# Turning the gate columns round and sending small factors through DRAM in a hybrid decoder layer

## The chip, the cores and the metric

The kernel runs on one core of a Trainium2 chip, as one program. A core has a matrix engine (TensorE, PE in the profile; its weight loads are PEld), VectorE (DVE), ScalarE (ACT), GpSimd (POOL) and SyncE (SP), which here only issues DMA transfers. The metric is device time in microseconds of one execution, median of several runs; smaller is better. All data is 32-bit floating point. TensorE multiplies operands in a reduced format, `fp32r`, so each operand is split into a high and a low part, and a product is three matmuls: high x high, high x low, low x high.

## The reference

One layer for 256 tokens of width 2048. A normalised x is projected by one wide matrix, and its columns feed three groups of heads (LRU, mLSTM, MoBA), each closed by a SiLU gate; then an output projection, cross-attention into 256 memory tokens, and a last norm. Cut to what the change touches:

```python
h = rms_norm(x, mix_norm_g)            # x * rsqrt(mean(x*x)) * g, one factor a token
p = h @ w_in
(lru_x, lru_z, ml_u, ml_o, ml_z, ml_i, ml_f, mo_q, mo_k, mo_v, mo_z) = jnp.split(p, SPLIT_POINTS, axis=-1)
# mLSTM, 4 heads
ig = ml_i + bi;  lf = log_sigmoid(ml_f + bf)
b = cumsum(lf);  m = running maximum of (ig - b), later b + m        # per head, over tokens
s = (q @ k.T) * exp(d - m) ...;  hn = layer_norm(sigmoid(ml_o) * num / den) * norm_g
y_ml = hn * silu(ml_z)
# MoBA, 6 heads, 256 tokens: one block, so causal softmax attention with a distance penalty
y_mo = softmax(q @ k.T * scale - slope * dist) @ v * silu(mo_z)
x = x + concat(y_lru, y_ml, y_mo) @ w_out
x = x + cross_attention(rms_norm(x), rms_norm(mem))
```

## The kernel before

The weights are cut into groups of columns (lx, u0, u1, o0, o1, q0, q1, k0, k1, z0, v0, v1, z1, z2, then out0 to out3, ck, cq, cv and wo), and each group into chunks of up to 128 x 1024 numbers (512 KB), numbered through the program: o0 is 24 to 31, o1 32 to 39, q0 40 to 47, q1 48 to 55, k0 56 to 63, k1 64 to 71, z0 72 to 79, v0 and v1 to 95, z1 96 to 103, z2 104 to 107.

Each chunk passes three stages. `load(i)` (L152, its DMA at L164) brings it into one of four `raw` buffers, from SyncE's queue. `split(i)` (L167) makes `wh` on ScalarE (L189) and `wl` on VectorE (through `tt`, L140), in six buffers each. `mm(i)` (L235) multiplies. Groups of kind "W" hold the weights still and move 256 token columns through TensorE (L251, L252, L254), so the result has channels on partitions. Groups of kind "X" hold the tokens still and move up to 512 weight columns (L266, L267, L268), so the result has tokens on partitions. 

The main loop over chunks emits the splits up to four chunks ahead and the loads another four ahead of those, then `mm(i)`. After a group's last chunk `done(group)` puts generators in a queue (evacuations in front, longer work behind), and after each chunk `step()` runs one step of the queue. So side work on VectorE and ScalarE stands in a row with the splits, and every engine works in the order in which the program names its instructions; nothing reorders them.

The work around the change: `square` and `stats` (L375, L388) make each token's 1/rms from squares on ScalarE, sums on GpSimd and two products on TensorE (L391, L400). `lru_core` (L422) has exponentials at L441 and L442 and a square root at L449. `o_evac` (L500) makes sigmoids (L507) and the raw mLSTM gates `if`. `ml_conv` (L487) runs four taps for each tile, three of them on VectorE as `w<-w,vec,w`. `ml_gates` (L511) makes the logarithm of the forget gate by `log1p` (L343), transposes the gates on TensorE to 4 rows of 256 tokens (L542, L543), scans them for the sum and the maximum (L545, L547) and transposes back (L556, L557); in the trace this begins at 138 us, in the chunks of q1. `ml_heads` spreads a head's maximum over partitions by matmuls with `nrow` (L610). `ml_z` and `mo_z` evacuate the SiLU gates, `ml_y` and `mo_y` multiply with them, in channels.

Of the kernel before, what the change touches and what calls it, by code (L numbers as in the profile page):

```python
# [97 lines left out]
def kernel(ctx: ExitStack, tc: tile.TileContext, xT, memT, x, mem, ws, vec_d, lw_d, fg_d, out):  # L98
# [274 lines left out]
    sq = {}  # L373

    def square(which, j):  # L375

        t = staged[which, j]
        if j == 0:
            sq[which] = small("mask", 512)
            S.activation(sq[which], t.rearrange("p a b -> p (a b)"), AF.Square)  # L380
        else:
            q = small("yt", 512)
            S.activation(q, t.rearrange("p a b -> p (a b)"), AF.Square)  # L383
            G.tensor_tensor(sq[which], sq[which], q, OP.add)  # L384
        if j == 7:
            G.tensor_tensor(sq[which][:, :256], sq[which][:, :256], sq[which][:, 256:], OP.add)

    def stats(which):  # L388
        p = ps()
        for t in range(2):  # L390
            P.matmul(p[:, t:t + 1], sq[which][:, t * 128:t * 128 + 128], ones[:, 0:1], start=True, stop=True)  # L391
# [2 lines left out]
        rstd_of(r, p[:, 0:2], D, RMS_EPS)
        d = small("yt", 512)[:, :256].rearrange("p (a b) -> p a b", a=2)
        for t in range(2):
            V.tensor_scalar(d[:, t, :], ident, r[:, t:t + 1], None, op0=OP.mult)
        yield
        p = ps()
# [732 lines left out]
```

## Time and profile before

| what | value |
|---|---|
| runs | 526.89, 526.77, 526.19 us |
| median | 526.77 us |
| the profiled execution | 527.48 us |
| its span in the trace | 525.8 us |
| TensorE's granted clock, mean | 0.995 |
| TensorE busy | 98% of the span |
| VectorE, ScalarE, GpSimd busy | 65%, 54%, 9% |

The trace covers 525.8 of the 527.48 us of its execution, and times in it count from the span's start. A row of a timeline has the start, the length, the engine, the line, the operation, what is written and read, the shape, a count, and in brackets how long the engine sat idle before it and who ended that. Lengths of TensorE's rows overlap, since its matmuls are pipelined: what a matmul costs is the distance from one start to the next. Where a helper such as `tt` makes the instruction, the line is the helper's, and the tile's name tells which one it is. Times of a chunk mean the start of its first matmul.

### The profile page before, as it was taken

The numbers are of one execution on the slowest core, as the hardware profiler recorded it, in microseconds if no ns is written. First come the engines' busy times: TensorE is split into PE (matmuls) and PEld (weight loads), VectorE is DVE, ScalarE is ACT, GpSimd is POOL, SyncE is SP. The second block draws the span as 40 slices with busy tenths as digits, with TensorE's granted clock in tenths as the row PEclk, the third lists the DMA queues.
The fourth block names the chain that finished last, engine by engine and source line by source line (L and its number), as shares of the span: only waits on it lengthen the run. The fifth ranks groups of instructions, "written<-read, shape, count | busy, mean of one in ns | idle before, by whom it ended". The sixth has DMA issues, their size and how long they took to land.

```text
span 525.8 us, 8864 instructions
## 1 busy us (share of the span) xinstructions
PE 514.1 (98%) x3498; PEld 485.3 (92%) x3498; DVE 339.3 (65%) x522; ACT 282.3 (54%) x424; POOL 47.6 (9%) x67
## 2 busy tenths in 40 slices
PE   7999999999999999999999999999999999999993
PEld 6999999999999999999999999888888899988883
DVE  5986937695567537376666775764667866337574
ACT  4864567578645323432556455544648564447343
POOL 7354000000000000000200000000142010000000
PEclk9999999999999999999999999999999999999998
DMA  8975445467454554634557326588685565633604
GB/s 290 340 266 183 155 119 156 151 199 239 134 187 165 168 161 151 201 108 134 154 177 268 111 95 225 175 295 302 204 277 164 197 199 172 204 110 122 228 13 160
DMA packets 30362, 96.73 MB, mean 184 GB/s; under 512 B 3312, under 2 KB 3696, under 8 KB 30320
## 3 DMA queue, kind: packets, MB, share of 16 engines
q1 hardware_dynamic: 30176, 96.02, 55.7%
q8 instruction: 27, 0.44, 0.3%
q14 instruction: 15, 0.12, 0.1%
q10 hardware_dynamic: 144, 0.14, 0.1%
HBM read 94.05 MB, written 2.10 MB: 183 GB/s over the span
## 4 chain that ended last, share of the span: by engine, by line
PE 53%; issue 41%; DMA 2%; POOL 1%; DVE 1%; ACT 0%; POOLq 0%; ACTq 0%; SPq 0%; DVEq 0%
PE acc_out L266 6%; PE acc_out L268 6%; PE acc_out L267 6%; PE acc_z L252 2%; PE acc_z L254 2%; PE acc_z L251 2%; PE acc_v L268 1%; PE acc_ck L254 1%; PE acc_cq L254 1%; PE acc_cq L252 1%; PE acc_cq L251 1%; PE acc_ck L252 1%; PE acc_ck L251 1%; PE acc_v L267 1%; PE acc_v L266 1%
## 5 line engine op out<-in xcount | busy, mean ns | idle before, releaser
L140 DVE TENSOR_TENSOR wl<-raw,wh 128x1024 fp32r<-128x1024 f32 (+3 forms) x166 | 197.3, 1198 | 100.6 <-ACT wh L189 99.0
L189 ACT ACTIVATE wh<-raw 128x1024 fp32r<-128x1024 f32 (+2 forms) x162 | 160.8, 1010 | 49.7 <-PE acc_k L252 12.8
L266 PE MATMUL acc_out<-wh,ah_y 128*128 128x512 f32 x128 | 50.8, 397 | 0.0
L268 PE MATMUL acc_out<-wh,al_y 128*128 128x512 f32 x128 | 49.9, 390 | 0.0
L267 PE MATMUL acc_out<-wl,ah_y 128*128 128x512 f32 x128 | 49.8, 389 | 0.0
L251 PE MATMUL acc_z<-ah_x,wh 128*128 128x256 f32 x160 | 46.6, 291 | 0.0
L254 PE MATMUL acc_z<-ah_x,wl 128*128 128x256 f32 x160 | 45.2, 283 | 0.0
L252 PE MATMUL acc_z<-al_x,wh 128*128 128x256 f32 x160 | 45.2, 283 | 0.0
L251 PE MATMUL acc_q<-ah_x,wh 128*128 128x256 f32 x128 | 37.2, 290 | 0.0
L251 PE MATMUL acc_k<-ah_x,wh 128*128 128x256 f32 x128 | 37.0, 289 | 0.0
L251 PE MATMUL acc_u<-ah_x,wh 128*128 128x256 f32 x128 | 36.8, 288 | 0.0
L254 PE MATMUL acc_u<-ah_x,wl 128*128 128x256 f32 x128 | 36.2, 283 | 0.0
L252 PE MATMUL acc_k<-al_x,wh 128*128 128x256 f32 x128 | 36.2, 283 | 0.0
L252 PE MATMUL acc_u<-al_x,wh 128*128 128x256 f32 x128 | 36.2, 283 | 0.0
L254 PE MATMUL acc_q<-ah_x,wl 128*128 128x256 f32 x128 | 36.2, 283 | 0.0
L254 PE MATMUL acc_k<-ah_x,wl 128*128 128x256 f32 x128 | 36.2, 283 | 0.0
L252 PE MATMUL acc_q<-al_x,wh 128*128 128x256 f32 x128 | 36.2, 283 | 0.0
L384 POOL TENSOR_TENSOR mask<-mask,yt 128x512 f32<-128x512 f32 x14 | 22.4, 1598 | 152.6 <-ACT yt L383 152.6
L252 PEld LDWEIGHTS acc_z<-al_x,wh 128*128 128x128 f32 x160 | 30.6, 192 | 0.2
L251 PEld LDWEIGHTS acc_z<-ah_x,wh 128*128 128x128 f32 x160 | 30.6, 192 | 0.2
L254 PEld LDWEIGHTS acc_z<-ah_x,wl 128*128 128x128 f32 x160 | 30.6, 191 | 0.0
L268 PEld LDWEIGHTS acc_out<-wh,al_y 128*128 128x128 f32 x128 | 24.0, 188 | 5.1
(286 smaller groups left out, 1291.0 us busy)
## 6 DMA issues: line engine op xcount, KB each, us to landing
raw<-ws SPq DMA_DIRECT2D x138, 512.0 KB, 4.0
raw<-ws SPq DMA_DIRECT2D x24, 384.0 KB, 3.1
raw<-ws SPq DMA_DIRECT2D x8, 392.0 KB, 3.2
w<-x SPq DMA_DIRECT2D x4, 512.0 KB, 6.5
w<-memT SPq DMA_DIRECT2D x8, 256.0 KB, 4.9
out<-xg SPq DMA_DIRECT2D x8, 256.0 KB, 3.0
w<-xT SPq DMA_DIRECT2D x7, 256.0 KB, 6.2
raw<-ws SPq DMA_DIRECT2D x4, 256.0 KB, 5.6
```

Source lines behind the costliest of these rows:

```text
L140: V.tensor_tensor(out, a, b, op)
L189: S.activation(h[:, :kc * n], r[:, :kc * n], AF.Copy)
L251: P.matmul(o, h[:, sl], mv_h, start=first and m % 2 == 0, stop=False, skip_group_check=True)
L252: P.matmul(o, h[:, sl], mv_l, start=False, stop=False, skip_group_check=True)
L254: P.matmul(o, l[:, sl], mv_h, start=False, stop=last, skip_group_check=True)
L266: P.matmul(o, xh[:, sl], mh, start=first, stop=False)
L267: P.matmul(o, xh[:, sl], ml, start=False, stop=False)
L268: P.matmul(o, xl[:, sl], mh, start=False, stop=last)
L384: G.tensor_tensor(sq[which], sq[which], q, OP.add)
```

## The change

Five things are changed.

The gate groups z0, z1 and z2 (and the two gate tiles that were in k1) become kind "X": weights move, and the gates come out with tokens on partitions. `gate_z` evacuates them by ScalarE alone, with 1/rms as a scale. The heads' outputs are multiplied with them token by token, and `to_channels` transposes the products on TensorE, for MoBA too; MoBA's values are made token by token, with the softmax's division folded into their evacuation.

The sums of squares come from loads of x and mem by rows (`row_load`, four of 512 KB each), squared and summed along the row on ScalarE; 1/rms is written to DRAM (256 numbers) and read back broadcast to all partitions.

The mLSTM gates move from the queue to a list `side` that is advanced after every chunk, beginning right after o0. Their transposes are replaced by DMA through DRAM: `d_if` is written, two transfers of 4 x 256 single numbers read it as `gates_in`; after the scans two such transfers write `d_gates`, which is read back as `acol`; the maximum is broadcast as `nrow` (512 KB). All of them are issued from SyncE's queue.

At the start, the first half of x's first tile is issued ahead of the first weights, `vec` comes in two pieces, and the high part of x's second tile is made by ScalarE. The load of `lw` moves from chunk 3 to chunk 6, and the LRU's evacuation comes one step later.

The core of the diff:

```diff
-    ("k1", "w_in", "W", "x", _cols(*_t(O_K, 4, 5), *_t(O_Z, 0, 1))),
-    ("z0", "w_in", "W", "x", _cols(*_t(O_Z, 2, 3, 4, 5))),
+    ("k1", "w_in", "W", "x", _cols(*_t(O_K, 4, 5))),
+    ("z0", "w_in", "X", "x", [(O_Z, 512)]),
...
-    ("z1", "w_in", "W", "x", _cols(*_t(O_MZ, 0, 1, 2, 3))),
-    ("z2", "w_in", "W", "x", _cols(*_t(O_MZ, 4, 5))),
+    ("z1", "w_in", "X", "x", [(O_Z + 512, 256), (O_MZ, 256)]),
+    ("z2", "w_in", "X", "x", [(O_MZ + 256, 512)]),
...
-            if which == "x" and j < 2:
+            if which == "x" and j < 1:
...
+    stage_load("x", xT, 0, (0, 1))
+    nc.scalar.dma_start(vec[:, :16], vec_d[:, :16])
     load(0, (0,))
-    stage_load("x", xT, 0, (0, 1))
-    nc.scalar.dma_start(vec, vec_d)
...
+    nc.sync.dma_start(vec[:, 16:], vec_d[:, 16:])
...
-        p = ps()
-        for t in range(2):
-            P.matmul(p[:, t:t + 1], sq[which][:, t * 128:t * 128 + 128], ones[:, 0:1], start=True, stop=True)
...
-        P.matmul(p[:, :256], ones[:, :128], d.rearrange("p a b -> p (a b)"), start=True, stop=True)
...
+    def row_load(which, src, i, tag):
+        rows[which, i] = big(tag, 1024)
+        t, c = i // 2, i % 2 * 1024
+        nc.sync.dma_start(rows[which, i], src[t * 128:t * 128 + 128, c:c + 1024])
+
+    def row_square(which, i):
+        t = rows[which, i]
+        S.activation(t, t, AF.Square, accum_out=ssq[which][:, i // 2, i % 2:i % 2 + 1])
...
+        V.reduce_sum(r, ssq[which], axis=AX.X)
+        rstd_of(r, r, D, RMS_EPS)
+        yield
+        d = drp.tile([2, 128], F32, name=f"d_{which}")
+        with nc.allow_non_contiguous_dma(reason="two numbers a token"):
+            nc.sync.dma_start(d.rearrange("t p -> p t"), r)
+        yield
         rr = small("rrow", 256)
         rrow[which] = rr
-        S.activation(rr, p[:, :256], AF.Copy)
+        nc.sync.dma_start(rr, d.rearrange("t p -> (t p)")[None, :].to_broadcast([128, 256]))
...
+        d = drp.tile([256, 8], F32, name="d_if")
+        nc.sync.dma_start(d.rearrange("(t p) c -> p t c", t=2), iff)
+        yield
+        w = selp.tile([4, 2, 256], F32, name="gates_in")
+        with nc.allow_non_contiguous_dma(reason="one number each"):
+            for a in range(2):
+                nc.sync.dma_start(w[:, a, :], d[:, 4 * a:4 * a + 4].rearrange("n h -> h n"))
...
+        o = selp.tile([4, 3, 256], F32, name="gates_out")
+        av, cb, ncm = (o[:, i, :] for i in range(3))
+        V.tensor_tensor_scan(cb, ones[:4, :], w[:, 1, :], 0.0, op0=OP.mult, op1=OP.add)
...
+        d, dn = drp.tile([256, 8], F32, name="d_gates"), drp.tile([4, 256], F32, name="d_nrow")
+        with nc.allow_non_contiguous_dma(reason="one number each"):
+            for a in range(2):
+                nc.sync.dma_start(d[:, 4 * a:4 * a + 4].rearrange("n h -> h n"), o[:, a, :])
+        nc.sync.dma_start(dn, o[:, 2, :])
+        yield
+        ac, nrow = small("acol", 2, 8), selp.tile([128, 4, 256], F32, name="nrow")
+        nc.sync.dma_start(ac, d.rearrange("(t p) c -> p t c", t=2))
+        nc.sync.dma_start(nrow, dn[None, :, :].to_broadcast([128, 4, 256]))
...
-            pn = ps()
-            for i in range(2):
-                P.matmul(pn[:, :256], M["sel"][:, h, :], M["nrow"][i], start=i == 0, stop=i == 1)
+            pn = M["nrow"][:, h, :]
...
+    def gate_z(group, a):
+
+        if group == "z0":
+            M["sz"] = big(6, 2, 768)
+            parts = [(0, 512, M["sz"], 0)]
+        elif group == "z1":
+            B["sz"] = big(2, 2, 768)
+            parts = [(0, 256, M["sz"], 512), (256, 512, B["sz"], 0)]
+        else:
+            parts = [(0, 512, B["sz"], 256)]
+        for t in range(2):
+            for c0, c1, dst, d0 in parts:
+                S.activation(dst[:, t, d0:d0 + c1 - c0], a[t][:, c0:c1], AF.Silu, scale=rstd["x"][:, t:t + 1])
...
+    def to_channels(src, c):
+
+        p = ps()
+        for cc in range(2):
+            for t in range(2):
+                P.transpose(p[:, cc * 256 + t * 128:cc * 256 + t * 128 + 128],
+                            src[:, t, (c + cc) * 128:(c + cc) * 128 + 128], ident)
+        return p
...
+            P.matmul(p[:, 0:128], pt[:, 0:128], v[:, 0, vs], start=True, stop=True)
+            P.matmul(p[:, 128:256], pt[:, 128:256], v[:, 0, vs], start=True, stop=False)
+            P.matmul(p[:, 128:256], pt[:, 256:384], v[:, 1, vs], start=False, stop=True)
+            for t in range(2):
+                S.activation(o[:, t, vs], p[:, t * 128:t * 128 + 128], AF.Copy, scale=RS[h][:, t:t + 1])
...
+        for g in side:
+            next(g, None)
...
-            bg(idle(4), stats("x"), lru_evac(a), call(softplus_lam), lru_core())
+            bg(idle(2), stats("x"), lru_evac(a), call(softplus_lam), lru_core())
...
-            bg(ml_gates())
+            side.append(ml_gates())
...
+        if 2 <= i < 6:
+            row_load("x", x, i - 2, i - 1)
+        if i == 6:
             nc.sync.dma_start(lw, lw_d)
-        while nsq < 8 and nsq < i - 1:
-            square("x", nsq)
-            nsq += 1
+        if 6 <= i < 10:
+            row_square("x", i - 6)
```

The order of instructions, at the three places where the prediction's steps lie. VectorE, the end of o0, before: the split of chunk 34 is ahead of these rows, `w` are three taps of the convolution, `wl_1228` is the split of chunk 35, `if` are the two gate evacuations, then follow chunks 36 and 37.

```order
L143 SCALAR_TENSOR_TENSOR w_1222<-w_795,vec,w_1222 128x256 x3
L140 TENSOR_TENSOR wl_1228<-raw_1147,wh_1227 128x768
L143 SCALAR_TENSOR_TENSOR if<-acc_o_1088,rstd_x,vec 128x8
L143 SCALAR_TENSOR_TENSOR if<-acc_o_1089,rstd_x,vec 128x8
L140 TENSOR_TENSOR wl_1252<-raw_1167,wh_1251 128x768
L143 SCALAR_TENSOR_TENSOR w_1222<-w_795,vec,w_1222 128x256 x3
L140 TENSOR_TENSOR wl_1276<-raw_1186,wh_1275 128x768
```

The taps ahead of `if` are what moves here. VectorE after, from the split of chunk 35 (`wl_1211`) to that of chunk 36 (`wl_1235`) and the first row of the forget gate's logarithm:

```order
L142 TENSOR_TENSOR wl_1211<-raw_1134,wh_1210 128x768
L145 SCALAR_TENSOR_TENSOR if<-acc_o_1072,rstd_x,vec 128x8
L145 SCALAR_TENSOR_TENSOR if<-acc_o_1073,rstd_x,vec 128x8
L142 TENSOR_TENSOR wl_1235<-raw_1153,wh_1234 128x768
L145 SCALAR_TENSOR_TENSOR lf_e<-if 128x8
```

No taps stand ahead of `if` any more. Five short rows further on, the end of the logarithm, the copy into `if`, the first taps and the split of chunk 37 (`wl_1290`):

```order
L145 SCALAR_TENSOR_TENSOR lf_q<-lf_q,lf_s_1260 128x8 x6
L145 SCALAR_TENSOR_TENSOR lf_q<-lf_q,lf_s 128x8
L358 TENSOR_SCALAR lf<-lf_q 128x8
L145 SCALAR_TENSOR_TENSOR lf<-if,lf 128x8
L528 COPY if<-lf 128x2x4
L145 SCALAR_TENSOR_TENSOR w_1284<-w_779,vec,w_1284 128x256 x3
L142 TENSOR_TENSOR wl_1290<-raw_1173,wh_1289 128x768
```

The ten short instructions of the logarithm now stand between the splits of chunks 36 and 37, and the copy for the DMA behind them. VectorE after, from the split of chunk 40 to that of chunk 41, where before there were three taps alone:

```order
L142 TENSOR_TENSOR wl_1361<-raw_1238,wh_1360 128x1024
L542 SCALAR_TENSOR_TENSOR gates_out<-ones,gates_in 4x256
L142 TENSOR_TENSOR gates_out<-gates_in,gates_out 4x256
L544 SCALAR_TENSOR_TENSOR gates_out<-ones,gates_out 4x256
L545 TENSOR_SCALAR gates_out<-gates_out 4x256
L142 TENSOR_TENSOR gates_out<-gates_out 4x256
L145 SCALAR_TENSOR_TENSOR w_1284<-w_779,vec,w_1284 128x256 x3
L142 TENSOR_TENSOR wl_1389<-raw_1293,wh_1388 128x1024
```

The five instructions on the gates stand ahead of the taps and of split 41, and the first of them reads `gates_in`, which comes by DMA.

SyncE, before, from load 41 on (a load waits until its `raw` buffer is free):

```order
L164 DMA raw_1279<-ws 128x1024
L164 DMA raw_1301<-ws 128x1024
L164 DMA raw_1323<-ws 128x1024
L164 DMA raw_1345<-ws 128x1024
L164 DMA raw_1367<-ws 128x1024
```

Nothing but weights stands in this stretch of the queue. SyncE, after, from load 41 (`raw_1293`) to the broadcast of `nrow`, behind which load 47 follows; 4x256x1 are single numbers:

```order
L166 DMA raw_1293<-ws 128x1024
L532 DMA d_if<-if 128x2x8
L166 DMA raw_1317<-ws 128x1024
L537 DMA gates_in<-d_if 4x256x1 x2
L166 DMA raw_1342<-ws 128x1024
L166 DMA raw_1364<-ws 128x1024
L166 DMA raw_1392<-ws 128x1024
L551 DMA d_gates<-gates_out 4x256x1 x2
L552 DMA d_nrow<-gates_out 4x256
L166 DMA raw_1419<-ws 128x1024
L555 DMA acol<-d_gates 128x2x8
L556 DMA nrow<-d_nrow 128x1024
```

`gates_in` waits for `d_if`, and `acol` for `d_gates`, with the loads behind them in the same queue.

ScalarE, before, around the LRU's SiLU gate (L461) up to the square root (L449); the exponentials of L441 and L442 stand ahead of these rows:

```order
L189 ACTIVATE wh_1082<-raw_945 128x784
L461 ACT_TABLE_LOAD
L461 ACTIVATE w_1102<-w_1102 128x512
L189 ACTIVATE wh_1105<-raw_985 128x784
L189 ACTIVATE wh_1124<-raw_1021 128x784
L189 ACTIVATE wh_1143<-raw_1055 128x784
L449 ACT_TABLE_LOAD
L449 ACTIVATE w_1012<-w_1012 128x1024
```

Three splits alone stand between the SiLU and the square root here. ScalarE, after, the same place:

```order
L461 ACT_TABLE_LOAD
L461 ACTIVATE w_1086<-w_1086 128x512
L191 ACTIVATE wh_1089<-raw_963 128x784
L441 ACT_TABLE_LOAD
L441 ACTIVATE w_1029<-w_947,nsp_125 128x256
L442 ACTIVATE w_1030<-w_947,sp_124 128x256
L441 ACTIVATE w_1029<-w_947,nsp_125 128x256
L442 ACTIVATE w_1030<-w_947,sp_124 128x256
L191 ACTIVATE wh_1111<-raw_1003 128x784
L191 ACTIVATE wh_1130<-raw_1039 128x784
L191 ACTIVATE wh_1149<-raw_1070 128x768
L449 ACT_TABLE_LOAD
```

The second four exponentials have come behind the SiLU and have a table load of their own. The table load of the sigmoids (L507) further down carried the wait for `if` before; now the first sigmoid carries it.

## Rows read from the trace of the kernel before

**Rows 1.** The page, busy time of each engine, share of the span, instructions.

```profile
PE 514.1 (98%) x3498; PEld 485.3 (92%) x3498; DVE 339.3 (65%) x522; ACT 282.3 (54%) x424; POOL 47.6 (9%) x67
```

**Rows 2.** Waits of TensorE: line, waited for: us in total, times, longest.

```profile
PE acc_lx L251 <- ACT wh L180: 1.3, 1, 1.3
...
PE acc_lx L254 <- DVE wl L140: 0.9, 2, 0.5
```

**Rows 3.** Timeline of TensorE, a chunk of each kind: start, length, instruction.

```profile
116.07 0.28 PE L251 MATMUL acc_q<-ah_x,wh 128*128 128x256 f32 x1
...
118.81 0.28 PE L254 MATMUL acc_q<-ah_x,wl 128*128 128x256 f32 x1
...
335.72 0.39 PE L266 MATMUL acc_out<-wh,ah_y 128*128 128x512 f32 x1
...
339.80 0.39 PE L266 MATMUL acc_out<-wh,ah_y 128*128 128x512 f32 x1
```

**Rows 4.** Timeline of TensorE, first matmuls of chunks 36 and 37.

```profile
107.75 0.33 PE L266 MATMUL acc_o<-wh,ah_x 128*128 128x384 f32 x1
...
109.83 0.33 PE L266 MATMUL acc_o<-wh,ah_x 128*128 128x384 f32 x1
```

**Rows 5.** Timeline of ScalarE: exponentials, square root, sigmoids, split of chunk 36.

```profile
75.48 1.28 ACT L441 ACT_TABLE_LOAD   x1
...
78.39 0.84 ACT L189 ACTIVATE wh<-raw 128x784 fp32r<-128x784 f32 x1
...
90.33 1.28 ACT L449 ACT_TABLE_LOAD   x1 [2.62 <-DVE w L143]
...
102.13 1.28 ACT L507 ACT_TABLE_LOAD   x1 [5.90 <-DVE if L143]
...
104.37 0.84 ACT L189 ACTIVATE wh<-raw 128x768 fp32r<-128x768 f32 x1
```

**Rows 6.** Timeline of VectorE, from the gates `if` to the split of chunk 37.

```profile
101.83 0.35 DVE L143 SCALAR_TENSOR_TENSOR if<-acc_o,rstd_x,vec 128x8 f32<-128x8 f32 x2
105.25 0.96 DVE L140 TENSOR_TENSOR wl<-raw,wh 128x768 fp32r<-128x768 f32 x1 [3.06 <-ACT wh L189]
106.12 1.52 DVE L143 SCALAR_TENSOR_TENSOR w<-w,vec,w 128x256 f32<-128x256 f32 x3
107.56 0.95 DVE L140 TENSOR_TENSOR wl<-raw,wh 128x768 fp32r<-128x768 f32 x1
```

**Rows 7.** Timeline of TensorE: the statistics of x, and chunk 13 behind them.

```profile
43.45 0.50 PE L391 MATMUL ps<-ones,mask 128*128 128x1 f32 x4
43.82 0.36 PE L251 MATMUL acc_u<-ah_x,wh 128*128 128x256 f32 x1
...
46.77 0.60 PE L400 MATMUL ps<-yt,ones 128*128 128x256 f32 x2
47.02 0.47 PE L251 MATMUL acc_u<-ah_x,wh 128*128 128x256 f32 x1
```

**Rows 8.** The page, DMA queues (packets, MB, share) and issues (KB, us to landing).

```profile
q1 hardware_dynamic: 30176, 96.02, 55.7%
...
q10 hardware_dynamic: 144, 0.14, 0.1%
...
out<-xg SPq DMA_DIRECT2D x8, 256.0 KB, 3.0
```

**Rows 9.** Timeline of VectorE, the split of chunk 13.

```profile
36.40 1.67 DVE L140 TENSOR_TENSOR wl<-raw,wh 128x1024 fp32r<-128x1024 f32 x1 [0.57 <-ACT wh L189]
```

**Rows 10.** Timeline of VectorE: the logarithm, the split behind it, the scans.

```profile
138.49 0.16 DVE L143 SCALAR_TENSOR_TENSOR lf_e<-if 128x8 f32<-128x8 f32 x1
...
141.69 1.22 DVE L140 TENSOR_TENSOR wl<-raw,wh 128x1024 fp32r<-128x1024 f32 x1
...
150.71 0.68 DVE L545 TENSOR_TENSOR_SCAN w<-ones,ps 4x256 f32<-4x256 f32 x1 [1.45 <-PE ps L543]
...
153.24 0.27 DVE L551 CAST nrow<-w 4x256 fp32r<-4x256 f32 x1
```

More of the change, by code (lines that the diff above doesn't have):

```diff
@@ L372 @@
     rrow = {}
[L373 to L386, printed above, removed]
+    ssq = {w: small(f"ssq_{w}", 2, 2) for w in "xm"}
+    rows = {}
+    def row_load(which, src, i, tag):
[5 more added lines that the diff above has]
+        S.activation(t, t, AF.Square, accum_out=ssq[which][:, i // 2, i % 2:i % 2 + 1])
     def stats(which):
[L389 to L391 removed]
         r = small(f"rstd_{which}", 2)
         rstd[which] = r
[L394 to L397, printed above, removed]
+        V.reduce_sum(r, ssq[which], axis=AX.X)
+        rstd_of(r, r, D, RMS_EPS)
         yield
[L399 to L400 removed]
+        d = drp.tile([2, 128], F32, name=f"d_{which}")
+        with nc.allow_non_contiguous_dma(reason="two numbers a token"):
+            nc.sync.dma_start(d.rearrange("t p -> p t"), r)
+        yield
         rr = small("rrow", 256)
         rrow[which] = rr
[L403 removed]
+        nc.sync.dma_start(rr, d.rearrange("t p -> (t p)")[None, :].to_broadcast([128, 256]))
+        yield
+        yield
     def rb(which):
@@ L526, in ml_gates @@
                             channel_multiplier=-1)
-        w = big(6, 4, 256)[:4]
-        sel = selp.tile([128, 4, 128], F32R, name="sel")
-        ones_r = ones[:, :128]
-        M["sel"] = sel
-        for h in range(4):
-            G.affine_select(sel[:, h, :], ones_r, pattern=[[0, 128]], compare_op=OP.is_equal, fill=0.0,
-                            base=-h, channel_multiplier=1)
-        nrow = [selp.tile([128, 256], F32R, name=f"nrow{i}") for i in range(2)]
-        for r in nrow:
-            G.memset(r.bitcast(F32), 0.0)
@@ L537, in ml_gates @@
-        M["nrow"] = nrow
-        yield HARD
-        yield HARD
-        p = ps()
-        for t in range(2):
-            P.transpose(p[:4, t * 128:t * 128 + 128], lf3[:, t, :], ident)
-            P.transpose(p[:4, 256 + t * 128:256 + t * 128 + 128], iff[:, t, 0:4], ident)
-        cb, av, cm, ncm = (w[:, i, :] for i in range(4))
-        V.tensor_tensor_scan(cb, ones[:4, :], p[:4, 0:256], 0.0, op0=OP.mult, op1=OP.add)
-        tt(av, p[:4, 256:512], cb, OP.subtract)
-        V.tensor_tensor_scan(cm, ones[:4, :], av, 0.0, op0=OP.mult, op1=OP.max)
@@ L548, in ml_gates @@
-        V.tensor_scalar(ncm, cm, -1.0, None, op0=OP.mult)
-        tt(cb, ncm, cb, OP.subtract)
-        nh, nl = (r[:4, :] for r in M["nrow"])
-        V.tensor_copy(nh, ncm)
-        tt(nl, ncm, nh.bitcast(F32), OP.subtract)
-        yield HARD
-        p = ps()
-        for t in range(2):
-            P.transpose(p[:, t * 8:t * 8 + 4], av[:, t * 128:t * 128 + 128], ident[:4, :4])
-            P.transpose(p[:, t * 8 + 4:t * 8 + 8], cb[:, t * 128:t * 128 + 128], ident[:4, :4])
-        p3 = p[:, :16].rearrange("p (a b) -> p a b", a=2)
@@ L565, in ml_qkv @@
+        enb = small("enb", 2, 4)
+        S.activation(enb, ac[:, :, 4:8], AF.Exp)
+        M["acol"], M["enb"], M["nrow"] = ac, enb, nrow
+        yield
     def ml_qkv():
@@ L739, in scores @@
             V.reciprocal(sm_, sm_)
[L740 to L741 removed]
+            RS[h] = sm_
         def transposes(h):
@@ L755, in values @@
             vs = slice(h * 128, h * 128 + 128)
-            P.matmul(p[:, 0:256], v[:, 0, vs], pt[:, 0:256], start=True, stop=False, skip_group_check=True)
-            P.matmul(p[:, 128:256], v[:, 1, vs], pt[:, 256:384], start=False, stop=True, skip_group_check=True)
-            V.tensor_copy(oT[:, h, :], p[:, 0:256])
+            P.matmul(p[:, 0:128], pt[:, 0:128], v[:, 0, vs], start=True, stop=True)
+            P.matmul(p[:, 128:256], pt[:, 128:256], v[:, 0, vs], start=True, stop=False)
+            P.matmul(p[:, 128:256], pt[:, 256:384], v[:, 1, vs], start=False, stop=True)
+            for t in range(2):
+                S.activation(o[:, t, vs], p[:, t * 128:t * 128 + 128], AF.Copy, scale=RS[h][:, t:t + 1])
         for n in range(10):
@@ L963, in mem_stats @@
     def mem_stats():
-        for j in range(10):
-            if j < 8:
-                stage_load("m", memT, j)
-            if j >= 2:
-                square("m", j - 2)
+        for j in range(8):
+            if j < 4:
+                row_load("m", mem, j, (1, 2, 1, 2)[j])
+            stage_load("m", memT, j)
+            if 2 <= j < 6:
+                row_square("m", j - 2)
             yield
-        yield from idle(2)
         yield from stats("m")
```

96 lines of the change are left out of this document (44 added, 52 removed).

## The prediction

> **What bounds the kernel now.** I read the page's busy shares first, then TensorE's waits, then its timeline. TensorE is busy 98% of the span [rows 1], and the table of what it waits for adds up to a few microseconds, all in the first 15 us [rows 2]. After that its matmuls follow each other at a fixed pitch. So a matmul less is worth its pitch, and work on another engine is worth nothing until it makes a weight chunk late.
>
> The pitch: in a chunk whose weights are stationary, 24 matmuls of 256 columns start from 116.07 to 118.81, 0.119 us each, and such a chunk takes 2.86 us; in a chunk whose weights move, 19 matmuls of 512 columns start from 335.72 to 339.80, 0.227 us each [rows 3]. A chunk of 384 columns takes 109.83 - 107.75 = 2.08 us [rows 4].
>
> The place that matters is the end of o0. `o_evac` puts two `if` instructions into VectorE's row of splits, and ScalarE waits 5.90 us for them [rows 5]; from there VectorE makes three convolution taps (1.44 us) and a split (0.87) for each chunk [rows 6], 2.31 us against TensorE's 2.08, and it is late already: the split of chunk 36 ends at 105.25 + 0.96 = 106.21, 1.5 us before its first matmul at 107.75 [rows 4, 6]. Elsewhere the splits are several microseconds ahead.
>
> **The change part by part.** All times are of the profiled execution (527.48 us, 0.71 above the median of 526.77); what is gained or lost is then put on the median.
>
> Gate groups turned round: z0, z1 and z2 are 10 tiles of 128 columns by 16 k-tiles by 3 matmuls. 480 x 0.119 to 0.120 = 57.6 us before, 240 x 0.227 = 54.5 after: 3.1 gained. The evacuations shrink to one ScalarE pass beside at least 3 us of slack; nothing there decides.
>
> Statistics: the first product of squares holds TensorE from 43.45 to 43.82, the broadcast of 1/rms from 46.77 to 47.02, with a late next start behind each [rows 7]; 0.85 us for x, as much for mem: 1.7 gained. An engine of the 16 moves 20.5 GB/s while it is busy (96.02 MB in 55.7% of 16 x 525.8 us [rows 8]). The four row loads of x that come instead (4 x 512 KB, 6.4 us on all 16, less 1.6 for the lw load that moves away) stand in SyncE's queue ahead of weights; the split of chunk 13 ends at 36.40 + 1.67 = 38.07, its matmul starts at 47.02 [rows 7, 9], so 9.0 us cover 4.8. If that cover were gone, up to 4.8 us.
>
> Small matmuls: 8 gate transposes and 8 `nrow` matmuls go (16 x 0.12 = 1.9), 12 MoBA transposes come (1.4 to 1.8, taken 1.6), the values cost 0.2 more; 0.1 gained. The 12 mLSTM transposes only move, from 258 us to the time of z1, where splits are ahead.
>
> Start: the vector table (134 KB) leaves the head of the queue, and half of a VectorE conversion goes to ScalarE. The shown waits are 1.3 and 0.9 us [rows 2]; nothing of before shows what is late next there, so between 0 and 2.2, and I take 0.8, because the weight halves still come one by one behind each other.
>
> Gain: 3.1 + 1.7 + 0.1 + 0.8 = 5.7 us, to a median of 521.1 if nothing is lost.
>
> The losses lie at chunks 36 to 45, in the clock of before (what is gained ahead moves TensorE and the splits alike, since the splits wait there for buffers that TensorE frees). The order of VectorE shows `if` without the taps ahead of it, so at 101.83 - 1.44 = 100.4 at the earliest [rows 6]. But the order of ScalarE puts the exponentials of the LRU one step later, behind a table switch: 78.39 - 75.48 = 2.9 us [rows 5]. The square root behind them waited 2.62 us for VectorE [rows 5], and VectorE waits for the exponentials, so I take the bound with all of it: `if` at 100.4 + 2.9 = 103.3. From there:
> - `if` 0.3 to 103.6; sigmoids 0.95 (2.24 with the table load, whose 1.28 now come before the wait [rows 5]); chunk 36: 0.84 on ScalarE and 0.88 on VectorE, 106.3, before 107.75.
> - The log1p chain of the forget gate now stands here: 141.69 - 138.49 = 3.2 [rows 10], then a copy of 0.2, the taps 1.44 and the split of chunk 37, 0.95: 112.2. TensorE wants it at 109.83: 2.4 lost.
> - Chunks 38 and 39 at 2.31 against 2.08 and chunk 40 (taps and a split of 1.14) at 2.58: 1.0 lost. VectorE is done at 119.4.
> - The scans, 153.24 - 150.71 = 2.53 [rows 10], taps and split before chunk 41: 5.1 against a chunk of 2.86: 2.25 lost.
>
> That is 5.6. Behind a waiting scan stand all later splits, so TensorE pays for the DMA as well: `gates_in` must have landed by 119.4. SyncE issues `d_if` behind load 41, whose raw buffer the split of chunk 37 frees (112.2), and it lands 2.2 us on: the outgoing 256 KB take 3.0 us [rows 8], less 0.8 for their bytes. That is 114.6; `gates_in` follows load 42 and that landing, 115.1, and is there at 117.3 if its single numbers cost nothing.
>
> The price of a 4-byte element stands in no row. From above: q10's 144 packets (1 KB each) took 0.1% of 16 engines, 8.4 us, 58 ns each [rows 8]; from below: 1 KB at 20.5 GB/s is 52 ns of that, so about nothing. I take 10 ns (an estimate: what is left, 6 ns, and the rounding of 0.1%, which reaches from 29 to 88), nearer to the lower end as these packets were nearly all bytes. Two transfers of 4 rows of 256; if 4 rows go to 4 engines, 256 each, 2 x 256 x 10 ns = 5.1 us. So `gates_in` lands at 122.4: 3.0 lost. The other pair, `d_gates`, is issued behind load 45 (split 41 at 127.5), lands at 134.9, `acol` at 137.2, and the exponential and split 45 end at about 140.2; TensorE wants 45 at about 141 after four chunks of 2.86 and the headwise products: 0.7 us of cover, nothing lost. Load 47 stands in SyncE's queue behind the waiting `acol`, lands 2.2 + 1.6 us after 134.9, and is wanted some 6 us after chunk 45: covered. Range for the DMA: 0 to 29.7 us a pair at 58 ns.
>
> Loss 5.6 + 3.0 = 8.6, gain 5.7: 2.9 slower, 529.7 us (own time 530.4).
>
> On this step the Trainium skill (DMA: Bandwidth & Descriptors, Rules for kernel authors) says that a strided last dimension becomes one descriptor for each element, and that a plain DMA with a rearranged pattern is the wrong way to transpose, with a factor of 19 against a transposing DMA. By this the change trades 8 matmuls of 0.12 us for a slow transfer. No run here shows that factor; by the rows a pair costs between 0 and 29.7 us, and the sum would be 526.7 to 578. The same page of the Trainium skill (Why a DMA increments its semaphore by 16 and not by 1) says that the slowest dimension that is not 1 sets the number of engines; by it there would be 4, as I took.
>
> **The rivals.** *Early gates, cheap elements (faster).* The exponentials fit into ScalarE's idle time: VectorE reaches `if` at 100.4, chunk 37 is split at 109.3 and not late, chunk 40 at 116.5 (0.4 late), the scans cost 2.25. With elements under 4 ns `gates_in` lands at 114.4 to 116.5 in time. 521.1 + 2.65 = 523.7; it decides from `if` before 100.9 on. For it: the idle 2.62 us. Against: the chain passes through VectorE and back.
>
> *In time (same).* The elements spread over 16 engines, 64 each, or cost under 4 ns: the pair takes 1.3 us, lands at 118.6 before 119.4, and only 5.6 is lost: 526.7. Early gates with 10 ns come to the same 526.7.
>
> *Dear elements (much slower).* From 20 ns on both pairs are late: 529.7 + 5.1 + 4.4 = 539.2 at 20 ns, 544.3 at 25, 549.5 at 30, 578 at 58. For it: q10's mean taken whole. Against: those packets carried 1 KB each.
>
> *The change doesn't do what it says*: the turned gates don't keep 0.227 us. Against it, every group of that kind in the trace does [rows 3]. It would take back 3.1: 532.8; it lies in the range.
>
> **How the numbers follow.** Forecast 0.40, early and cheap 0.25, in time 0.18, dear 0.14, the rest (gates at the old pitch, row loads that make weights late) 0.03. A measurement of this kernel tells about 0.2%, 1.05 us, from no change. Faster 0.25 + 0.02 from the lower edge of "in time" = 0.27; same 0.18 - 0.02 + 0.02 from the lower edge of the forecast = 0.18; slower 0.38 + 0.14 + 0.03 = 0.55. The range goes down to 522.0, where the early case loses only 0.9, and up to 544.0, at 25 ns; outside are dear elements above that (0.09) and a case without loss (0.07). The forecast's own range is 527.8 to 534.
>
> **What would show it.** Right: TensorE waits before chunk 37 (about 2 us) and before chunk 41 (about 5), named on VectorE's `wl` split; VectorE waits for `gates_in` about 3 us in front of its first scan; the z groups show 0.227 us; the waits of [rows 2] are shorter. Wrong: `if` before 101 us; `gates_in` landing before VectorE asks; a longest wait at `acol` or `enb` around chunk 45; waits at chunks 9 to 16 (row loads).

## The result and the profile after

The changed kernel takes 541.47 us (median of four runs, 539.63 to 544.0), the kernel before 526.83: ratio 1.0279, 95% interval 1.025 to 1.0308. The direction was forecast, the size was not: 529.7 was said, +2.9 us; it is +14.6 us.

The profiled execution took 540.51 us, 13.0 more than that of the kernel before, span 538.6. TensorE's last matmul starts at 530.0 instead of 517.5 us. Cut at the first matmul of a group, the 12.5 us lie like this (us for each stretch; three of the experiments beside):

| stretch | before | after | e4 | e9 | e12 |
|---|---|---|---|---|---|
| start to u0 | 31.9 | 31.2 | 32.5 | 30.7 | 31.1 |
| u0, u1 | 50.4 | 51.6 | 50.4 | 50.7 | 49.6 |
| o0, o1 | 33.8 | 38.2 | 33.8 | 33.8 | 33.8 |
| q0, q1 | 53.8 | 66.3 | 53.8 | 54.1 | 54.1 |
| k0 to z2 | 156.3 | 151.4 | 153.5 | 151.4 | 151.4 |
| out0 to the last matmul | 191.3 | 191.3 | 193.0 | 191.2 | 192.1 |

What TensorE waited for, after (engine line, waited for: us in total, times, longest); before there were waits in the first 15 us alone [rows 2]:

```profile
PE acc_q L256 <- DVE wl L142: 7.9, 1, 7.9
PE acc_o L269 <- DVE wl L142: 2.7, 1, 2.7
PE ps L591 <- issue: 1.9, 1, 1.9
PE acc_u L253 <- DVE w L142: 1.9, 1, 1.9
PE ps L298 <- DVE half L338: 1.3, 1, 1.3
PE acc_lx L253 <- ACT wh L182: 0.8, 1, 0.8
```

Four waits are new: in front of u1 (1.9), in chunk 37 (2.7), in chunk 41 (7.9) and at chunk 45 (1.9). VectorE's timeline of the changed kernel shows the middle two, and answers [rows 6] and [rows 10]:

```profile
104.29 0.35 DVE L145 SCALAR_TENSOR_TENSOR if<-acc_o,rstd_x,vec 128x8 f32<-128x8 f32 x2
...
107.24 0.16 DVE L145 SCALAR_TENSOR_TENSOR lf_e<-if 128x8 f32<-128x8 f32 x1
...
110.84 1.52 DVE L145 SCALAR_TENSOR_TENSOR w<-w,vec,w 128x256 f32<-128x256 f32 x3
112.27 0.95 DVE L142 TENSOR_TENSOR wl<-raw,wh 128x768 fp32r<-128x768 f32 x1
...
119.19 1.22 DVE L142 TENSOR_TENSOR wl<-raw,wh 128x1024 fp32r<-128x1024 f32 x1
126.93 0.68 DVE L542 TENSOR_TENSOR_SCAN gates_out<-ones,gates_in 4x256 f32<-4x256 f32 x1 [6.51 <-DMA gates_in<-d_if]
...
130.88 1.22 DVE L142 TENSOR_TENSOR wl<-raw,wh 128x1024 fp32r<-128x1024 f32 x1
```

The split of chunk 37 starts at 112.27, behind the logarithm and the taps. VectorE is ready for the scan at 120.4 and stands 6.51 us, because `gates_in` lands at 126.9. SyncE's timeline shows where the transfers begin, and how long their issue holds the queue (second column):

```profile
113.63 0.43 SPq L532 DMA_DIRECT2D d_if<-if  x1
...
116.81 3.40 SPq L537 DMA_DIRECT2D gates_in<-d_if  x2
...
132.50 4.27 SPq L551 DMA_DIRECT2D d_gates<-gates_out  x2
136.82 3.94 SPq L552 DMA_DIRECT2D d_nrow<-gates_out  x1
...
144.48 0.39 SPq L555 DMA_DIRECT2D acol<-d_gates  x1
```

The first transfer of a pair is issued within 0.4 us. What is issued next takes 3 to 4 us, be it the second of the pair, the write of `d_nrow`, which is in rows, or a load of weights. Behind `gates_in` such a load takes 4.17 us to issue, and from 119 to 125 the core's DMA moves 1 GB/s (last column of the second row):

```profile
120.31 4.17 SPq L166 DMA_DIRECT2D raw<-ws  x1
...
119.00:125.00 6.00, 5.24 (x39) 5.04 (x37) 1.41 (x2) 3.50 (x4) 0.00 (x0) 1.00 0.34 1
```

The wait at chunk 45, which the table of waits puts down to "issue", is one for `acol`: on ScalarE the split of chunk 45 and the evacuations that TensorE needs stand behind an exponential that waits 9.0 us for it.

```profile
148.77 0.21 ACT L560 ACTIVATE enb<-acol 128x8 f32<-128x8 f32 x1 [9.00 <-DMA acol<-d_gates]
```

A table by stretches (length, busy time of each engine with its instructions, granted clock, DMA share, GB/s) shows a loss that no wait names:

```profile
113.00:117.00 4.00, 3.72 (x13) 3.73 (x14) 3.86 (x9) 0.78 (x2) 0.00 (x0) 0.57 0.56 151
117.00:120.00 3.00, 3.00 (x19) 3.00 (x19) 2.93 (x5) 1.24 (x2) 0.00 (x0) 1.00 0.59 155
...
132.00:138.00 6.00, 5.85 (x27) 5.74 (x28) 3.83 (x6) 4.40 (x6) 0.00 (x0) 0.57 0.49 88
138.00:148.00 10.00, 10.00 (x79) 9.79 (x78) 1.23 (x1) 1.75 (x2) 0.00 (x0) 1.00 0.54 82
```

Behind each of the two long waits the granted clock is mostly at its lower level (0.50, 1.2 of 2.4 GHz), 0.57 on the mean. TensorE's timeline has it as a pitch, 0.32 us for 384 columns (0.173 before) and 0.21 for 256 (0.119):

```profile
113.28 0.69 PE L269 MATMUL acc_o<-wl,ah_x 128*128 128x384 f32 x1 [2.66 <-DVE wl L142]
...
114.08 0.52 PE L268 MATMUL acc_o<-wh,ah_x 128*128 128x384 f32 x1
114.40 0.52 PE L269 MATMUL acc_o<-wl,ah_x 128*128 128x384 f32 x1
...
132.15 0.58 PE L256 MATMUL acc_q<-ah_x,wl 128*128 128x256 f32 x1 [7.91 <-DVE wl L142]
132.53 0.41 PE L253 MATMUL acc_q<-ah_x,wh 128*128 128x256 f32 x1
132.75 0.41 PE L254 MATMUL acc_q<-al_x,wh 128*128 128x256 f32 x1
```

From 113.28 to 116.64 ten pitches take 3.36 us instead of 1.73, from 132.15 to 137.01 twenty-two take 4.86 instead of 2.62: 1.6 and 2.2 us.

The wait in front of u1 begins at the factors of x. SyncE with what it waits for, VectorE and TensorE:

```profile
41.62 0.39 SPq L397 DMA_DIRECT2D d_x<-rstd_x  x1
...
50.10 0.33 SPq L401 DMA_DIRECT2D rrow<-d_x  x1
...
SPq L401 <- DMA d_x<-rstd_x: 6.7, 1, 6.7
...
55.39 1.29 DVE L142 TENSOR_TENSOR w<-acc_lx,rrow 128x512 f32<-128x512 f32 x2 [9.22 <-DMA rrow<-d_x]
...
56.23 0.36 PE L253 MATMUL acc_u<-ah_x,wh 128*128 128x256 f32 x1 [1.85 <-DVE w L142]
```

A write of 256 numbers is issued at 41.62, and the read-back waits for it until 50.10; it lands at 55.4. Only then is the accumulator of lx evacuated, which u1 needs.

The turned gates did as forecast; chunks 68 and 69 answer [rows 3]: from 227.39 to 232.63, 23 pitches, 0.228 us each.

```profile
227.39 0.40 PE L268 MATMUL acc_z<-wh,ah_x 128*128 128x512 f32 x1
...
232.63 0.39 PE L270 MATMUL acc_z<-wh,al_x 128*128 128x512 f32 x1
```

### The profile page after: what moved, and what is told of

Its sections match the earlier page's. It is cut to its first block, busy times and chain, and to the rows that moved or that the text cites. A ratio compares the mean times of both kernels' runs of the same rounds, so it can differ in the third digit from the quotient of the medians.

```text
span 538.6 us, 8260 instructions
## 1 busy us (share of the span) xinstructions
PE 513.4 (95%) x3206; PEld 473.3 (88%) x3206; DVE 321.5 (60%) x495; ACT 287.5 (53%) x437; POOL 24.5 (5%) x45
## 4 chain that ended last, share of the span: by engine, by line
PE 78%; DMA 7%; issue 6%; DVE 4%; POOL 3%; ACT 1%; SPq 0%; POOLq 0%; ACTq 0%; DVEq 0%
PE acc_out L268 5%; PE acc_out L270 5%; PE acc_out L269 5%; PE acc_z L270 4%; PE acc_z L268 4%; PE acc_z L269 4%; PE acc_q L256 3%; PE acc_q L254 3%; PE acc_q L253 3%; PE acc_k L254 2%; PE acc_k L253 2%; PE acc_k L256 2%; PE acc_v L268 2%; PE acc_v L270 2%; PE acc_v L269 2%
## 5 line engine op out<-in xcount | busy, mean ns | idle before, releaser
L268 PE MATMUL acc_out<-wh,ah_y 128*128 128x512 f32 x128 | 50.7, 396 | 0.0
L268 PE MATMUL acc_z<-wh,ah_x 128*128 128x512 f32 x96 | 39.4, 410 | 0.0
L270 PE MATMUL acc_z<-wh,al_x 128*128 128x512 f32 x96 | 37.5, 391 | 0.0
L269 PE MATMUL acc_z<-wl,ah_x 128*128 128x512 f32 x96 | 37.5, 391 | 0.0
L256 PEld LDWEIGHTS acc_q<-ah_x,wl 128*128 128x128 f32 x128 | 25.6, 200 | 8.1 <-DVE wl L142 8.1
L269 PEld LDWEIGHTS acc_out<-wl,ah_y 128*128 128x128 f32 x128 | 24.1, 188 | 4.7
L268 PEld LDWEIGHTS acc_out<-wh,ah_y 128*128 128x128 f32 x128 | 24.1, 188 | 4.7
L253 PE MATMUL acc_k<-ah_x,wh 128*128 128x256 f32 x96 | 27.7, 289 | 0.0
L254 PE MATMUL acc_k<-al_x,wh 128*128 128x256 f32 x96 | 27.2, 283 | 0.0
L256 PE MATMUL acc_k<-ah_x,wl 128*128 128x256 f32 x96 | 27.1, 283 | 0.0
L253 PEld LDWEIGHTS acc_u<-ah_x,wh 128*128 128x128 f32 x128 | 24.6, 192 | 2.1 <-issue 2.0
```

The source lines that it names most:

```text
L253: P.matmul(o, h[:, sl], mv_h, start=first and m % 2 == 0, stop=False, skip_group_check=True)
L254: P.matmul(o, h[:, sl], mv_l, start=False, stop=False, skip_group_check=True)
L256: P.matmul(o, l[:, sl], mv_h, start=False, stop=last, skip_group_check=True)
L268: P.matmul(o, xh[:, sl], mh, start=first, stop=False)
L269: P.matmul(o, xh[:, sl], ml, start=False, stop=False)
L270: P.matmul(o, xl[:, sl], mh, start=False, stop=last)
```

## The experiments

**Which part costs what.** Theory A: four separate stalls, each from a step of the change that leaves the engines' covers; theory B: one of them drags the others along.

e1 undoes the statistics.

```diff
-        V.reduce_sum(r, ssq[which], axis=AX.X)
...
-            nc.sync.dma_start(d.rearrange("t p -> p t"), r)
...
+            P.matmul(p[:, t:t + 1], sq[which][:, t * 128:t * 128 + 128], ones[:, 0:1], start=True, stop=True)
...
+        P.matmul(p[:, :256], ones[:, :128], d.rearrange("p a b -> p (a b)"), start=True, stop=True)
```

> The changed kernel with the two statistics made as before (squares of the channel-major tiles, sums on GpSimd, products on TensorE). Theory A, the four stalls are separate: only the stall before the u1 group goes (2.0 us in the changed kernel's trace), the statistics of x cost 0.85 us again, so about 540.3 us, with the waits before chunks 37 and 41 where they are. Theory B, the 9.2 us that VectorE waited for the broadcast factor are what makes the gates late: the wait before chunk 37 (2.7 us and a slow clock behind it) goes too, about 536.

Measured 544.16 us (542.8 to 546.28), ratio 1.0334 [1.0308, 1.036]: neither. The stall before u1 is gone, and chunks 37 and 41 still wait, so B falls:

```profile
PE acc_q L256 <- DVE wl L142: 6.7, 1, 6.7
PE ps L594 <- ACT qh L586: 3.4, 1, 3.4
PE acc_o L269 <- DVE wl L142: 2.0, 1, 2.0
```

But the old statistics don't fit the new surroundings: 1.1 us at the end of lx and 1.4 in ck come new (e4 shows why), and the stall at chunk 45 grew from 1.9 to 3.4, with the lower clock behind it (0.50 from 148 to 152).

e2 undoes the way of the gates and keeps their place.

```diff
-                nc.sync.dma_start(w[:, a, :], d[:, 4 * a:4 * a + 4].rearrange("n h -> h n"))
...
+            P.transpose(p[:4, t * 128:t * 128 + 128], lf3[:, t, :], ident)
+            P.transpose(p[:4, 256 + t * 128:256 + t * 128 + 128], iff[:, t, 0:4], ident)
```

> The changed kernel with the mLSTM gates transposed on TensorE and spread by matmuls again, the scans left in their new place between the splits of chunks 40 and 41. Theory A, the wait before chunk 41 is mostly the DMA: it falls from 7.9 to about 2.3 us, its slow clock from 2.3 to about 1, the stall at chunk 45 (2.0) goes, the small matmuls cost 1.9: about 534. Theory B, the place alone costs it: the wait at chunk 41 stays over 5 us, about 539 or more.

Measured 537.05 us (532.93 to 540.12), 1.0169 [1.0111, 1.0228], between the two theories. The wait at chunk 41 is 2.7 us, near A's 2.3, and none is left at chunk 45: of the 7.9 us, about 5 are the transfer, 2.7 the place. The profiled execution, the slowest of the four, lost more elsewhere: 2.8 us before u1, and 2.6 in ck, where the factors of mem come by the same way.

e3 keeps the way and moves the place.

```diff
     def ml_gates():
-        yield
+        for _ in range(11):
+            yield
```

> The changed kernel with one edit: the gates' list begins 10 chunks later, with all its DMA through DRAM. Theory A, the transfer costs only where the splits are short of slack: the waits before chunks 37, 41 and 45 and their slow clock (4.3 + 10.4 + 2.0 us) go, about 525. Theory B, the single-number transfers hold up the weight loads wherever they stand, or their 10 us reach past the slack of the later chunks (7 us): about 530 to 536, with the wait moved to chunks 47 to 56.

Measured 528.33 us over ten runs (525.1 to 531.5), 1.0029 [1.0003, 1.0055]: 13 us come back by one line. The waits at chunks 37, 41 and 45 are gone. 525 was not reached: 2.0 us before u1 stay, with 0.52 of the full clock from 58 to 60 us behind them, and a part moved to the end of q1, where SyncE stood in the gates' writes and a load came late (1.7 and 0.8). So both theories hold in part: the place decides, and the writes hold up weights even there.

**What the other parts bring.** e4 leaves statistics and gates as before; gate groups, values and start are changed.

```diff
-            side.append(ml_gates())
+            bg(ml_gates())
...
-            pn = M["nrow"][:, h, :]
...
+                P.matmul(pn[:, :256], M["sel"][:, h, :], M["nrow"][i], start=i == 0, stop=i == 1)
```

(and the statistics as in e1)

> The gate groups with weights moving, the token-major values and the new start alone; statistics and mLSTM gates as in the kernel before. Theory A, these parts gain what was forecast for them, 3.1 + 0.8 us less 1.6 + 0.2 for transposes and values: about 524.6. Rival, the turned gates cost as much elsewhere (the evacuation, more transposes at the end of the MoBA heads): 526 to 527, no difference.

Measured 526.75 us, 1.0002 [0.9992, 1.0011]: the rival. But the gain is there and given back: k0 to z2 takes 2.8 us less, the start 0.8 less up to 28 us. ScalarE's timeline and waits show two new debts:

```profile
25.85 0.63 ACT L386 ACTIVATE yt<-w 128x512 f32<-128x512 f32 x1 [4.18 <-POOL mask L387]
```

```profile
ACT yt L811 <- PE ps L403: 9.3, 1, 9.3
```

GpSimd's first sum of squares now stands behind its block-diagonal constants, which start at 12 us instead of 4, since their part of the vector table comes later (1.1 us of TensorE in lx). And the queue of side work is longer, so the broadcast of mem's factors comes two chunks later on TensorE, while ScalarE has run ahead and waits (1.4 us in ck).

e5 mends both.

```diff
-        if i == 0:
+        if i == 14:
             late_consts()
...
-        yield from idle(2)
         yield from stats("m")
```

> The version with statistics and gates as before (526.75 us) with two edits: the block-diagonal constants on GpSimd are made after chunk 14 instead of after chunk 0, and two idle steps ahead of the statistics of mem go. Theory A, its gain was given back at two places, 1.1 us before a chunk of lx, where ScalarE waits 4.2 us for a sum on GpSimd that stands behind the late constants, and 0.9 + 0.5 us in ck, where ScalarE waits 9.3 us for TensorE's broadcast: about 524.6. Rival, the stalls move to another place: 526 to 527.

Measured 525.59 us, 0.998 [0.9971, 0.999], between the theories. Both stalls went; one of 0.8 us took their place, TensorE waiting for GpSimd's last sum of mem. e11 keeps one idle step:

```diff
-        yield from stats("m")
+        yield from idle(1)
+        yield from stats("m")
```

> The version with gates and statistics on TensorE and both covers restored (525.6 us), with one idle step kept ahead of the statistics of mem, since without any TensorE waited 1.0 us for GpSimd's last sum. Expected 524.7; rival, the wait moves to ScalarE as with two steps: 525.6 to 526.

Measured 524.99 us, 0.9964 [0.995, 0.9978]. So without any trip through DRAM the change is worth 1.9 us.

**What is slow in the trip.** e6 is e3 with the factors of x and mem turned on TensorE and written as rows.

```diff
-            nc.sync.dma_start(d.rearrange("t p -> p t"), r)
...
+        P.transpose(p[:2, :128], r, ident)
...
+        V.tensor_copy(rt, p[:2, :128])
+        nc.sync.dma_start(d, rt)
```

> The version with the gates 10 chunks later (528.3 us), and the factor of x and of mem transposed on TensorE and written to DRAM as two rows of 512 bytes instead of 256 single numbers; the way back by broadcast stays. Theory A, the 256 small writes themselves hold up the memory for 8 us: VectorE's wait for the broadcast falls from 9.2 to about 3.5 us, the stall before u1 (2.2 us and 1.3 of slow clock) goes, about 524.8. Rival, the round trip through DRAM costs it, whatever the form of the write: the stall stays over 1.5 us, about 528.

Measured 526.24 us (523.89 to 527.36), 0.9981 [0.9962, 0.9999]. VectorE's wait for the broadcast fell from 9.2 to 5.6 us, not to the 3.5 forecast, and the stall before u1 is gone: A in the main, 1.4 us short of its time. At the start of k0 TensorE still waits 0.8 + 0.7 us. The runs lie in two groups, 523.9 to 524.5 and 526.0 to 527.4; the profiled one (524.02) is of the lower.

e8 measures the writes by themselves, on the kernel before.

```diff
+                nc.sync.dma_start(d.rearrange("t p -> p t"), rstd["x"])           # chunk 58, 1 KB
+                nc.sync.dma_start(d[:, :, 0].rearrange("t p -> p t"), rstd["x"])  # 66, 256 bytes apart
+                nc.sync.dma_start(d.rearrange("n h -> h n"), ones[:4, :64])       # 74, from 4 partitions
+                nc.sync.dma_start(d, ones[:2, :128])                              # 82, two rows
+                nc.sync.dma_start(d.rearrange("n h -> h n"), ones[:4, :256])      # 90, 1024 numbers
```

> The kernel before with five extra writes to DRAM, one each behind chunks 58, 66, 74, 82 and 90, that nothing reads: 256 single numbers from 128 partitions side by side in 1 KB; the same 256 numbers 256 bytes apart; 256 numbers from 4 partitions into 1 KB; 256 numbers as two rows; 1024 numbers from 4 partitions into 4 KB. Theory A, many engines writing single numbers into the same 1 KB stop the memory: after the first one the weight loads stand still for 6 to 9 us, after the second and the fourth for less than 1 us. Rival, each single number costs the same wherever it goes: the first three stop alike, the fifth four times as long.

One run, 537.36 us. The first two writes differ only in the distance of their numbers, and land 10.2 and 3.1 us after their issue (last column):

```profile
p_dense<-rstd_x SPq DMA_DIRECT2D x1, 1.0 KB, 10.2
p_apart<-rstd_x SPq DMA_DIRECT2D x1, 1.0 KB, 3.1
```

The stretches in which weights are loaded behind each write (columns as above; the last two are DMA share and GB/s), in the same order:

```profile
182.00:186.00 4.00, 4.00 (x33) 4.00 (x33) 2.07 (x2) 1.06 (x1) 0.00 (x0) 1.00 0.80 75
210.00:213.00 3.00, 3.00 (x25) 3.00 (x24) 2.13 (x2) 1.06 (x1) 0.00 (x0) 1.00 0.71 199
236.00:243.00 7.00, 7.00 (x60) 7.00 (x59) 6.01 (x18) 1.03 (x2) 0.00 (x0) 1.00 0.87 70
258.00:261.00 3.00, 3.00 (x20) 2.96 (x20) 2.15 (x4) 1.86 (x4) 0.00 (x0) 1.00 0.71 214
278.00:291.00 13.00, 13.00 (x97) 12.90 (x97) 2.17 (x2) 0.53 (x1) 0.00 (x0) 1.00 1.09 58
```

Where the numbers lie side by side, weights move at 58 to 75 GB/s while the DMA engines are as busy as ever (0.80 to 1.09): a packet takes long. This ends some 10 us after the issue of 256 numbers (174.9 to 185, 232.6 to 243) and 17 us after that of 1024 (274.1 to 291). With 256 bytes between them, or as rows, the loads run at 199 and 214. Between 179 and 182 and between 207 and 210 no weights moved, so what the first two writes do to loads in that time isn't seen. That the numbers come from 128 partitions isn't needed: the third and the fifth come from 4. Whether several engines are needed, as A has it, is not shown. The rival falls with the second; its second half falls with the fifth, whose slow stretch is twice as long (13 us against 7), not four times.

e9 puts this into the gates: e6 with the scans' results written as rows, and the transposition left to the read.

```diff
-                nc.sync.dma_start(d[:, 4 * a:4 * a + 4].rearrange("n h -> h n"), o[:, a, :])
-        nc.sync.dma_start(dn, o[:, 2, :])
...
+        nc.sync.dma_start(do, o)
...
+                    nc.sync.dma_start(ac[:, t, 4 * a:4 * a + 4], do[:, a, t * 128:t * 128 + 128].rearrange("h p -> p h"))
```

> The version with late gates and row-wise statistics (526.2 us), where the scanned gates are written to DRAM as four contiguous rows too, and the transposition is left to the read: 128 partitions fetch 16 single numbers each. Theory A, single numbers hold things up when they are written side by side, not when they are read: SyncE's queue, which stood 8.0 us in the two writes, is free after less than 1 us, the stall at the start of k0 (1.8 us) goes, about 524.4. Rival, single numbers cost the same when they are read: the stall stays, 526.

Measured 522.32 us (522.24 to 522.36), 0.9912 [0.9897, 0.9927], 2.1 better than forecast, and the runs no longer scatter. The write's issue takes 0.33 us instead of 4.27 + 3.94, and 2048 numbers are read in single pieces by 128 partitions, with what stands behind them issued in 0.5 us each. Not every read is like that: `gates_in` still goes into 4 rows, and the load behind it takes 4.10 us to issue, as in the changed kernel, but here TensorE does not wait for it.

```profile
139.61 4.10 SPq L166 DMA_DIRECT2D raw<-ws  x1
...
149.97 0.33 SPq L553 DMA_DIRECT2D d_gates<-gates_out  x1
...
153.45 2.74 SPq L559 DMA_DIRECT2D acol<-d_gates  x4
```

TensorE's waits behind the start are down to one:

```profile
PE ps L298 <- DVE half L338: 1.3, 1, 1.3
PE acc_lx L256 <- DVE wl L142: 1.0, 2, 0.8
PE ps L397 <- POOL rstd_x L344: 0.9, 1, 0.9
```

e10 makes that edit in the changed kernel, gates in their early place.

```diff
-                nc.sync.dma_start(d[:, 4 * a:4 * a + 4].rearrange("n h -> h n"), o[:, a, :])
...
+        nc.sync.dma_start(do, o)
```

> The changed kernel with that edit alone: scanned gates written as rows, transposed by the read, in their early place. Theory A, the waits before chunks 37 (2.7 us) and 41 (7.9) stay, since they come before that write, and the stall at chunk 45 (1.9) goes: about 539. Rival, the write also made chunk 41 late, since chunks behind it were short of loads: 536 or less.

Measured 537.2 us (536.57 to 540.94), 1.0209 [1.0172, 1.0246]. The waits at chunks 37 (2.7) and 41 (7.6) stay, the one at chunk 45 is gone: A. The gain of 4.3 is over the 2.5 forecast. In the profiled executions it is 2.7, 1.9 at chunk 45 and 0.8 from a shorter wait before u1; the rest lies within what the runs of both scatter.

**The clock.** e7 fills the two waits of the changed kernel.

```diff
+        if i in (36, 40):
+            for _ in range(6 if i == 36 else 18):
+                P.matmul(pf[:, :256], ones[:, :128], ones, start=True, stop=True)
```

> The changed kernel with 6 matmuls of the constant ones (0.43 us each) added behind chunk 36 and 18 behind chunk 40, whose products nothing reads: TensorE works where it waited. Theory A, the granted clock falls because TensorE idles: the matmuls behind chunks 37 and 41 keep their pitch of 0.173 and 0.120 us instead of 0.32 and 0.21, and it is about 3.5 us faster than the changed kernel, 538. Rival, the clock falls there for another reason: no gain, 541 to 542.

Measured 543.61 us, 1.0308 [1.0285, 1.033]. The clock did what A says, the time didn't (granted clock in the third column from the right):

```profile
113.00:118.00 5.00, 4.93 (x26) 4.28 (x25) 4.58 (x16) 4.24 (x7) 0.00 (x0) 1.00 0.18 64
...
126.00:137.00 11.00, 10.33 (x58) 9.19 (x57) 6.14 (x12) 1.01 (x2) 0.00 (x0) 1.00 0.38 104
...
156.00:160.00 4.00, 4.00 (x24) 4.00 (x24) 2.45 (x2) 3.95 (x8) 0.00 (x0) 0.63 0.81 275
```

With TensorE working, the clock stays at 1.00 behind both places. But the next step still waits for `acol`, whose read-back is issued 13.0 us behind the write instead of 12.0, so the wait at chunk 45 grew from 1.9 to 5.0 us, with the slow clock behind it. The 1.6 + 2.2 us of slow matmuls lay ahead of a later wait, which took them. The profiled execution is the slowest of the four, and its wait before u1 is 3.3 us instead of 1.9, so what the filling itself costs is not shown; a gain of 3.5 us is not there.

**A version better than both.** e12 is e9 with e5's later constants.

```diff
-        if i == 0:
+        if i == 14:
             late_consts()
```

> The version with late gates and all writes as rows (522.3 us), with the block-diagonal constants on GpSimd made after chunk 14 instead of after chunk 0. Its one stall left behind the start is 0.9 us at 39 us, where TensorE's transposition of 1/rms waits for GpSimd, which stands in those constants; with 0.1 us of late start behind it the trace shows 1.06. Expected 521.3; rival, the wait is taken over by another one: 522.3.

Measured 521.61 us (520.82 to 522.42), 0.9895 [0.9878, 0.9911] against the kernel before. The wait for GpSimd is gone (u0 and u1 take 49.6 us), but the profiled execution, the slowest of the four, gave 0.9 back behind out0, so it can't be told from e9.

## Why the prediction was right or wrong

**The bound.** Right: TensorE's waits and slow matmuls, 1.9 before u1, 2.7 + 1.6 at chunk 37, 7.9 + 2.2 at chunk 41 and 1.9 at chunk 45, are 18.2 us; less a gain of about 6 they are the 12.5 but for some tenths.

**The gain, forecast 5.7.** Near: 0.75 at the start (0.8), 0.8 in the statistics of x (0.85), 4.9 from k0 to z2. e4 parts the last: 2.8 for gates and values (3.1 - 0.2 forecast). Of the other 2.1, six `nrow` matmuls are 0.7, and 1.2 is no gain: the scores of one head, which with early gates stand ahead of k0. The 12 MoBA transposes stand behind out0 (from 344 us, 1.1 us). There they hide the 0.85 for mem, and out0 to the end is as long as before. That the start costs nothing elsewhere was not argued: its table was also GpSimd's, and with the old statistics that takes the gain back (e4).

**`if` at 103.3, chunk 37 split at 112.2, 2.4 us late.** Right, and by the way that was said: o0 starts 0.5 us later here than before, so these are 103.8 and 112.7; `if` came at 104.29, the split ended at 113.22, and the wait was 2.7. The chain of small steps, replayed from rows of before, held to a microsecond over ten instructions. The 1.0 us for chunks 38 to 40 shows as no wait: TensorE was slower there itself.

**The price of a number, 10 ns.** The size was near and the step was wrong. Packets of 4 bytes take 9 ns in the trace's records (median). But reading `gates_in` took from 116.8 to 126.9, 10.1 us instead of 7.3, 3.4 of them the issue on SyncE, so VectorE waited 6.5 us, not 3.0; what makes this read so long, no run here separates. And a write was priced like a read, by its packets alone. `d_gates` is issued at 132.5 and its read-back at 144.5: 12.0 us instead of 7.3, so the 0.7 us of cover was gone, and chunk 45 waited. e8 and e9 show the reason: written side by side, numbers slow other traffic; read by 128 partitions, they don't. Read into 4 rows they hold up the load behind them, too, by 4 us.

**The factors of x.** This term failed most plainly. Four row loads were costed, and no wait in u0 is theirs. The 256 single writes of `d_x` were put at nothing; they take 8.5 us to the read-back, and the whole trip 13.8. The slack of TensorE there (9 us) covers splits; but u1 waits for lx's accumulators, and the sum has no term for that. e1 and e6 take this stall away, each in its own way.

**The clock, not in the sum.** 1.6 + 2.2 us of slow matmuls stand behind the two long waits. Each wait was priced as its length. The Trainium skill (TensorE: Matmul & The Clock Gate, Why this matters for your kernels) warns of idle gaps between bursts of matmuls, since TensorE goes on at half rate behind them; the traces agree, 0.57 behind the waits and 1.00 where e7 filled them. But e7 was no faster, so the term would not simply add.

**The rivals.** "Dear elements" gave the time (541.5 lies at 22 ns by its sum) for a wrong reason, so the nearness is luck: numbers took about 9 ns, and the wait before u1 and the slow clock, some 5.7 us together, are in no rival. "In time" is closest to e3, by another way: not cheaper numbers, but a later place.
